# Input projection: one 512-column matmul against the high and low halves of x for the product in bank 3, with the halves added in the gathering

## The chip, the cores and the metric

The kernel runs on one core of a Trainium2 chip. The metric is the device time of one execution in microseconds (us); lower is better. The kernel before takes 1921.91 us (median of three runs, 1921.67 to 1923.59).

## The reference

Two layers are computed for 512 positions of width 2048: a pooling mixer and a multi-head latent attention. The change lies in the first matrix product of the mixer:

```python
def pool_mixer_layer(x, norm_g, w_in, w_group, scale, w_out):
    h = rmsnorm(x, norm_g)
    proj = h @ w_in                      # 512 x 2048 times 2048 x 8192
    u, gate = proj[..., :W_A], proj[..., W_A:]
    ...                                  # causal mean pooling of u in four groups
    y = jnp.einsum('bsgc,gcd->bsgd', pooled, w_group).reshape(B, S, W_A) * scale
    y = y * jax.nn.silu(gate)
    return x + y @ w_out
```

All of it is float32. The kernel keeps that precision with two rounded halves of every operand, high and low, and three products: high weights by high x, high weights by low x, low weights by high x.

## The kernel before, in words

**The input projection** works on *pairs* of output tiles (two times 128 output columns, all 512 positions). It treats a pair and the two halves of the positions (H = 256) as a two-by-two block product and needs seven products instead of eight, of combined weights and combined x (a Strassen-Winograd scheme). Thirty pairs are done this way; two more were done plainly, in the stretch ahead, while the combined x were made.

- `w_combos(pair, q)` loads raw weights, combines them on VectorE (DVE, line 308) and GpSimd (POOL, lines 310 and 311), casts the seven high parts on ScalarE (ACT, line 314: `hi`) and subtracts for the low parts on DVE (line 315: `lo`). `hi` and `lo` have two buffers each, so the cast for one group of weights waits until TensorE (PE) has finished the group two before it. A pair has four such groups, q = 0 to 3; each serves two values of j.
- `seven(ks, w, j)` issues for each of the seven products three matmuls of 256 columns: lines 333 (high weights, high x), 335 (high weights, low x) and 337 (low weights, high x). The table `SEVEN` says which weight, which x, which PSUM bank and which half of that bank. Banks 0, 1 and 2 hold two products each, one in either half. Bank 3 holds one, in half 0, the fourth of the seven; its half 1 stays idle. `ps7` holds two sets of four banks, used by turns.
- `gather(ks, pair)` adds the seven sums: an ACT copy of bank 2's half 0 (line 343), then four DVE additions (lines 344 to 347); line 346 reads bank 3. Pairs are then stored to DRAM, or pooled first (`pool_tile`).

**Behind the last pair** comes the next stage: for each group, products of the pooled tiles (`at`, cast on ACT and subtracted on DVE, line 149) with the group weights (`whi` and `wlo`, lines 126 and 127), matmul lines 144 to 146, 24 of them for each of eight outputs `o`. Each load of weights serves 12 matmuls. DVE also scales the gate tiles read back from DRAM there (line 454). I call the start of the first of these matmuls, right behind the last pair, the *handover*.

**The order** on each engine is set by a scheduler that runs a model of the timeline while the program is built; it places each instruction where its model finds it ready. Engines then work strictly in that order. The code of all stages is scheduled together, so the end of one stage and the start of the next interleave.

Of the kernel before, what the change touches and what calls it, by code (L numbers as in the profile page):

```python
# [11 lines left out]
ALU = mybir.AluOpType  # L12
AX = mybir.AxisListType

P = 128
# [32 lines left out]
def trunk_kernel(  # L48
# [17 lines left out]
    V, A, G, T = nc.vector, nc.scalar, nc.gpsimd, nc.tensor  # L66
# [12 lines left out]
    def at(dt=F32R, shape=(P, S)):  # L79
        return apool.tile(list(shape), dt, tag="a", name="at")  # L80

    def bt(shape=(P, S), dt=F32R):
        return bpool.tile(list(shape), dt, tag="b", name="bt")
# [19 lines left out]
    def dram():  # L103
        return dpool.tile([P, S], F32, tag="scr", name="scr", bufs=64)
# [46 lines left out]
    def gsplit(src, gcol, hi, lo):  # L151
        g = cs[:, gcol:gcol + 1]
        A.activation(hi, src, AF.Copy, scale=g)
        V.scalar_tensor_tensor(lo, src, g, f(hi), ALU.mult, ALU.subtract)
# [73 lines left out]
    H = 256  # L228
    NJ = KD // 2
# [5 lines left out]
    def pool_tile(src, neg, w):  # L235

        up = tt_(PAD + S)
        G.memset(up[:, 0:PAD], 0.0)
        if len(src.shape) == 3:
            dst, r = (a.rearrange("p (h t) -> p h t", h=2) for a in (up[:, PAD:], ra[0]))  # L240
        else:
            dst, r = up[:, PAD:], ra[0]
        V.scalar_tensor_tensor(dst, src, -1.0 if neg else 1.0, r, ALU.mult, ALU.mult)
        prev, off = up, PAD
        m = 1
        while m < w:
            ext = w - 2 * m
            nw = S + ext
            nx = tt_(PAD + S)
            V.tensor_tensor(nx[:, 0:nw], prev[:, off - ext:off + S],  # L250
                            prev[:, off - ext - m:off + S - m], ALU.add)
            prev, off = nx, ext
            m *= 2
        s = prev

        V.scalar_tensor_tensor(s[:, 0:w - 1], s[:, 0:w - 1], float(w), cs[:, C_RCNT:C_RCNT + w - 1],
                               ALU.mult, ALU.mult)
        pl = tt_()
        V.scalar_tensor_tensor(pl, s[:, 0:S], 1.0 / w, up[:, PAD:], ALU.mult, ALU.subtract)
        return pl  # L260

    with ExitStack() as c1:
# [3 lines left out]

        ps7 = [c1.enter_context(tc.tile_pool(name=f"ps7{i}", bufs=1, space=bass.MemoryType.PSUM, **tile_))
               for i in range(2)]
        xh, xl = [None] * NJ, [None] * NJ

        def x_load(j):

# [4 lines left out]
        def x_parts(j, c, hp):  # L277

            nc.sync.dma_start(c[:, 0:2, :], xT[2 * j + 1].rearrange("p (h t) -> p h t", h=2))
            hl = xcp[j].tile([P, 2, 7, H], F32R, tag="xc", name="xc")  # L280
            h, lo = hl[:, 0], hl[:, 1]
            xh[j], xl[j] = h, lo
            h12 = hp.tile([P, H], F32R, tag="h12", name="h12", bufs=NJ)
            l12 = hp.tile([P, H], F32R, tag="l12", name="l12", bufs=NJ)
            gsplit(c[:, 2, :], C_GA + 2 * j, h[:, 2, :], lo[:, 2, :])
            gsplit(c[:, 7, :], C_GA + 2 * j, h12, l12)
            gsplit(c[:, 0:2, :], C_GA + 2 * j + 1, h[:, 0:2, :], lo[:, 0:2, :])
            return h12, l12
# [31 lines left out]
        def banks(n):  # L320
            return [ps7[n % 2].tile([P, 2, H], F32, tag=f"k{i}", name=f"k{i}") for i in range(4)]
# [5 lines left out]
        def seven(ks, w, j):  # L327
            hi, lo = w
            for wi, xi, b, h in SEVEN:
                dst = ks[b][:, h, :]  # L330
                first, last = j == 0 and h == 0, j == NJ - 1

                T.matmul(dst, hi[:, j % 2, wi, :], xh[j][:, xi, :], start=first, stop=False,  # L333
                         skip_group_check=True)
                T.matmul(dst, hi[:, j % 2, wi, :], xl[j][:, xi, :], start=False, stop=False,  # L335
                         skip_group_check=True)
                T.matmul(dst, lo[:, j % 2, wi, :], xh[j][:, xi, :], start=False, stop=last,  # L337
                         skip_group_check=True)

        def gather(ks, pair):  # L340

            e = epool.tile([P, 7, H], F32, tag="e", name="e")
            A.copy(e[:, 6, :], ks[2][:, 0, :])
            V.tensor_tensor(e[:, 0:2, :], e[:, 6:7, :].broadcast_to([P, 2, H]), ks[0], ALU.add)
            V.tensor_tensor(e[:, 2, :], e[:, 1, :], ks[2][:, 1, :], ALU.add)
            V.tensor_tensor(e[:, 3:6:2, :], e[:, 1:3, :], ks[3][:, 0:1, :].broadcast_to([P, 2, H]), ALU.add)
            V.tensor_tensor(e[:, 4:7:2, :], e[:, 2:4, :], ks[1], ALU.add)
            for i, v in enumerate((e[:, 0:7:6, :], e[:, 4:6, :])):
                o = 2 * pair + i
                raws[o] = dram()  # L350
                if i:
                    neg.add(o)
                if o < 8:
                    nc.sync.dma_start(raws[o], pool_tile(v, i == 1, WINS[0]))
                else:
                    nc.sync.dma_start(raws[o].rearrange("p (h t) -> p h t", h=2), v)
# [3 lines left out]
        with ExitStack() as c2:  # L360
            hp = c2.enter_context(tc.tile_pool(name="hp", bufs=2, **tile_))
            for j in range(NJ):
                c4 = ExitStack()
                if j == 0:
                    c4.enter_context(tc.high_priority())
                c = x_load(j)
                raw = hp.tile([P, 4, 2, P], F32, tag="hraw", name="hraw")
                hi = w7.tile([P, 4, 2, P], F32R, tag="hi", name="hi")
                lo = w7.tile([P, 4, 2, P], F32R, tag="lo", name="lo")
                parts = None  # L370
                for m in (0, 2):
                    for o in (m, m + 1):
                        nc.sync.dma_start(raw[:, o, :, :], awin[32 + o][:, 2 * j * P:2 * (j + 1) * P].rearrange(
                            "p (k n) -> p k n", k=2))
                    parts = parts or x_parts(j, c, hp)
                    split(raw[:, m:m + 2], hi[:, m:m + 2], lo[:, m:m + 2])
                h12, l12 = parts
                c4.close()
                x_sums(j, c)
                a, b = xh[j], xl[j]  # L380
                for o in range(4):
                    for dst, k, h, l in ((accs[o][:, 0, :], 0, a[:, 2, :], b[:, 2, :]),
                                         (accs[o][:, 1, :], 0, h12, l12),
                                         (accs[o], 1, a[:, 0:2, :], b[:, 0:2, :])):
                        first = j == 0 and h is not h12 and k == 0
                        T.matmul(dst, hi[:, o, k, :], h, start=first, stop=False, skip_group_check=True)
                        T.matmul(dst, hi[:, o, k, :], l, start=False, stop=False, skip_group_check=True)
                        T.matmul(dst, lo[:, o, k, :], h, start=False, stop=j == NJ - 1 and k == 1,
                                 skip_group_check=True)
        epool = c1.enter_context(tc.tile_pool(name="epool", bufs=2, **tile_))  # L390
        tp[0] = c1.enter_context(tc.tile_pool(name="tpool1", bufs=6, **tile_))
        for o in range(0, 4, 2):
            e = epool.tile([P, 7, H], F32, tag="e", name="e")
# [18 lines left out]
        for n, pair in enumerate((*range(18, 32), *range(16))):  # L412
            ks = banks(n)
            for q in range(NJ // 2):
                w = w_combos(pair, q)
                seven(ks, w, 2 * q)
                seven(ks, w, 2 * q + 1)
            if 0 < n < 9:
                squares(2 * n - 2)
            if n == 9:  # L420
                V.tensor_tensor(sq[0], sq[0], sq[1], ALU.add)
                p = ps7[0].tile([P, 2, H], F32, tag="k3", name="k3").rearrange("p h t -> p (h t)")
                ra[0] = norm_r(sq[0], D, p)
            gather(ks, pair)
# [41 lines left out]
    for g in range(NG):  # L466
# [11 lines left out]
        for o in range(KD):  # L478
            first = len(wloads)
# [15 lines left out]
    for k in range(KD):  # L495
        hi, lo = at(), at()
        gsplit(xr[k], C_GKV + k, hi, lo)
        xkv.append((hi, lo))
        hi, lo = bt(), bt()
# [45 lines left out]
    for k0 in range(0, KD, 4):  # L545
# [7 lines left out]
        for j in range(4):  # L553
            k = k0 + j
            xh, xl = xkv[k]
# [497 lines left out]
    for m in range(len(seq) + 2):  # L1053
        now = seq[m] if m < len(seq) else None
        if now:
            hg, h, i = now
# [26 lines left out]
    for ins in block[begin:]:  # L1083
        e = ins.engine
# [77 lines left out]
```

## Time and profile before

| | before |
|---|---|
| median of three runs | 1921.91 us |
| the profiled execution, its own time | 1925.17 us |
| its span | 1923.4 us |
| granted TensorE clock | 1.00 |
| first matmul of the thirty pairs | 53.8 us |
| first matmul of the next stage | 662.01 us |
| VectorE busy over the span | 66% |
| ScalarE busy over the span | 42% |
| matmuls of lines 333, 335, 337 | 1680 each |

Times of rows count from the span's start. A row of the timeline gives start, duration (both us), engine, line, operation, the tiles written and read, and in brackets how long the engine sat idle before it and what ended that. The span leaves out 1.8 us of the profiled execution's own time.

### The profile page before, as it was taken

How to read it: one execution, taken by the hardware profiler on the slowest of the kernel's cores; microseconds unless marked ns; L12 is line 12 of the kernel's file. 1: busy time of each engine (PE TensorE's matmuls, PEld its weight loads, DVE VectorE, ACT ScalarE, POOL GpSimd, SP SyncE). 2: the span in 40 equal slices, each digit the busy share in tenths (PEclk: the TensorE clock that was granted, in tenths of full speed). 3: DMA queues.
4: the chain of work that ended last, by engine and by line, in shares of the span. 5: the costliest groups of instructions: out<-in, count | busy, mean ns of one | idle time of the engine just before them, and what ended most of it. 6: DMA issues, size and time to landing. Idle time of an engine off the chain costs nothing.

```text
span 1923.4 us, 30647 instructions
## 1 busy us (share of the span) xinstructions
PE 1905.5 (99%) x11324; PEld 1701.2 (88%) x11324; DVE 1277.0 (66%) x2252; ACT 816.1 (42%) x1525; POOL 280.6 (15%) x436
## 2 busy tenths in 40 slices
PE   8999999999999999999999999999999999999999
PEld 7999999999999988888888888888888888988887
DVE  8677785797666777486595566564335988887332
ACT  8443433333333433233333354233235787785221
POOL 0433333343222100000000000000001232320000
PEclk9999999999999999999999999999999999999999
DMA  6454444344444446344344344234343222234632
GB/s 191 154 165 155 153 130 134 121 130 136 147 146 135 159 154 213 116 126 146 112 132 137 105 148 137 89 93 126 118 124 95 82 92 71 81 123 147 202 117 88
DMA packets 177079, 251.27 MB, mean 131 GB/s; under 512 B 15776, under 2 KB 96800, under 8 KB 176928
## 3 DMA queue, kind: packets, MB, share of 16 engines
q1 hardware_dynamic: 176640, 249.10, 41.2%
q8 instruction: 89, 1.46, 0.3%
q14 instruction: 62, 0.51, 0.1%
q10 hardware_dynamic: 288, 0.20, 0.0%
HBM read 216.21 MB, written 33.03 MB: 130 GB/s over the span
## 4 chain that ended last, share of the span: by engine, by line
PE 89%; DVE 4%; DMA 3%; ACT 1%; issue 1%; SPq 0%; POOL 0%; DVEq 0%; ACTq 0%; POOLq 0%
PE mm L144 15%; PE mm L146 15%; PE mm L145 15%; PE k L337 10%; PE k L335 10%; PE k L333 10%; PE sc L789 2%; PE mm L641 1%; PE mm L642 1%; PE mm L643 1%; PE mm L664 1%; PE mm L666 1%; PE mm L665 1%; PE tr L817 1%; PE tr L755 1%
## 5 line engine op out<-in xcount | busy, mean ns | idle before, releaser
L126 ACT CAST whi<-raw 128x512 fp32r<-128x512 f32 (+2 forms) x424 | 255.7, 606 | 514.3 <-PE mm L145 428.8
L333 PE MATMUL k<-xc,hi 128*128 128x256 f32 x1680 | 460.1, 283 | 0.0
L335 PE MATMUL k<-xc,hi 128*128 128x256 f32 x1680 | 460.0, 283 | 0.0
L127 DVE TENSOR_TENSOR wlo<-raw,whi 128x512 fp32r<-128x512 f32 (+2 forms) x424 | 283.3, 669 | 239.5 <-ACT whi L126 236.5
L337 PE MATMUL k<-xc,lo 128*128 128x256 f32 x1680 | 417.8, 283 | 1.6 <-DVE lo L315 1.6
L146 PE MATMUL mm<-bt,wlo 128*128 128x512 f32 x944 | 368.1, 390 | 1.1 <-DVE wlo L127 1.1
L144 PE MATMUL mm<-bt,whi 128*128 128x512 f32 x944 | 367.7, 390 | 0.0
L145 PE MATMUL mm<-bt,whi 128*128 128x512 f32 x944 | 367.2, 389 | 0.0
L314 ACT CAST hi<-raw 128x1792 fp32r<-128x1792 f32 x120 | 202.8, 1690 | 365.0 <-PE k L337 252.8
L315 DVE TENSOR_TENSOR lo<-raw,hi 128x1792 fp32r<-128x1792 f32 x120 | 249.0, 2075 | 158.7 <-ACT hi L314 158.6
L333 PEld LDWEIGHTS k<-xc,hi 128*128 128x128 f32 x1680 | 322.5, 192 | 0.2 <-ACT hi L314 0.2
L335 PEld LDWEIGHTS k<-xc,hi 128*128 128x128 f32 x1680 | 322.5, 192 | 0.0
L337 PEld LDWEIGHTS k<-xc,lo 128*128 128x128 f32 x1680 | 296.8, 192 | 2.7 <-DVE lo L315 2.2
L146 PEld LDWEIGHTS mm<-bt,wlo 128*128 128x128 f32 x944 | 177.2, 188 | 38.8 <-DVE wlo L127 1.5
L144 PEld LDWEIGHTS mm<-bt,whi 128*128 128x128 f32 x944 | 177.3, 188 | 37.1 <-issue 0.2
L145 PEld LDWEIGHTS mm<-bt,whi 128*128 128x128 f32 x944 | 177.3, 188 | 36.3
L145 PE MATMUL mm<-at,whi 128*128 128x512 f32 x432 | 169.0, 391 | 0.6 <-DVE at L149 0.6
L146 PE MATMUL mm<-at,wlo 128*128 128x512 f32 x432 | 168.5, 390 | 0.5 <-DVE wlo L127 0.5
L144 PE MATMUL mm<-at,whi 128*128 128x512 f32 x432 | 168.9, 391 | 0.0
L310 POOL TENSOR_TENSOR raw<-raw 128x256 f32<-128x256 f32 x120 | 98.5, 821 | 436.9 <-DVE raw L308 414.1
L311 POOL TENSOR_TENSOR raw<-raw 128x256 f32<-128x256 f32 x120 | 102.7, 856 | 9.2
L145 PEld LDWEIGHTS mm<-at,whi 128*128 128x128 f32 x432 | 81.1, 188 | 18.6 <-DVE at L149 2.1
(1133 smaller groups left out, 2535.6 us busy)
## 6 DMA issues: line engine op xcount, KB each, us to landing
raw<-awin SPq DMA_DIRECT2D x240, 256.0 KB, 3.3
raw<-awo SPq DMA_DIRECT2D x128, 256.0 KB, 2.8
raw<-bwin SPq DMA_DIRECT2D x80, 256.0 KB, 2.8
raw<-awg SPq DMA_DIRECT2D x64, 256.0 KB, 2.8
scr<-e SPq DMA_DIRECT2D x56, 256.0 KB, 2.7
raw<-bwo SPq DMA_DIRECT2D x56, 256.0 KB, 2.8
raw<-wkvb SPq DMA_DIRECT2D x32, 256.0 KB, 3.0
raw<-wqb SPq DMA_DIRECT2D x32, 192.0 KB, 2.4
```

The costliest lines, as they stand in the source:

```text
L126: A.copy(hi[:, :n], raw[:, :n])
L127: V.tensor_tensor(lo[:, :n], raw[:, :n], f(hi[:, :n]), ALU.subtract)
L144: T.matmul(dst, wh, xh, start=first, stop=False)
L145: T.matmul(dst, wh, xl, start=False, stop=False)
L146: T.matmul(dst, wl, xh, start=False, stop=last)
L310: G.tensor_tensor(c[:, :, 6, :], c[:, :, 4, :], c[:, :, 2, :], ALU.add)
L311: G.tensor_tensor(c[:, :, 7, :], c[:, :, 6, :], c[:, :, 3, :], ALU.add)
L314: A.copy(hi, c[:, :, 1:8, :])
L315: V.tensor_tensor(lo, c[:, :, 1:8, :], f(hi), ALU.subtract)
L333: T.matmul(dst, hi[:, j % 2, wi, :], xh[j][:, xi, :], start=first, stop=False, skip_group_check=True)
L335: T.matmul(dst, hi[:, j % 2, wi, :], xl[j][:, xi, :], start=False, stop=False, skip_group_check=True)
L337: T.matmul(dst, lo[:, j % 2, wi, :], xh[j][:, xi, :], start=False, stop=last, skip_group_check=True)
```

## The change

For bank 3, high weights now meet high and low x in one matmul of 512 columns: the high part fills half 0 of the bank, the low part the half that was idle. The moving operand is `xhl[j][:, :, xi, :]`, two runs of 256 columns from the high and the low half of the x tile, which lie 7 x 256 elements apart. The third matmul (low weights) still adds to half 0. `gather` copies bank 3's half 1 to SBUF on ACT (new line 348), adds half 0 to it on DVE (new line 351), and the addition that read bank 3 (now line 352) reads that sum from SBUF.

```diff
-        xh, xl = [None] * NJ, [None] * NJ
+        xh, xl, xhl = [None] * NJ, [None] * NJ, [None] * NJ
...
-            xh[j], xl[j] = h, lo
+            xh[j], xl[j], xhl[j] = h, lo, hl
...
-                T.matmul(dst, hi[:, j % 2, wi, :], xh[j][:, xi, :], start=first, stop=False,
-                         skip_group_check=True)
-                T.matmul(dst, hi[:, j % 2, wi, :], xl[j][:, xi, :], start=False, stop=False,
-                         skip_group_check=True)
+                if b == 3:
+                    T.matmul(ks[3], hi[:, j % 2, wi, :], xhl[j][:, :, xi, :], start=first, stop=False,
+                             skip_group_check=True)
+                else:
+                    T.matmul(dst, hi[:, j % 2, wi, :], xh[j][:, xi, :], start=first, stop=False,
+                             skip_group_check=True)
+                    T.matmul(dst, hi[:, j % 2, wi, :], xl[j][:, xi, :], start=False, stop=False,
+                             skip_group_check=True)
...
             A.copy(e[:, 6, :], ks[2][:, 0, :])
+            A.copy(e[:, 4, :], ks[3][:, 1, :])
             V.tensor_tensor(e[:, 0:2, :], e[:, 6:7, :].broadcast_to([P, 2, H]), ks[0], ALU.add)
             V.tensor_tensor(e[:, 2, :], e[:, 1, :], ks[2][:, 1, :], ALU.add)
-            V.tensor_tensor(e[:, 3:6:2, :], e[:, 1:3, :], ks[3][:, 0:1, :].broadcast_to([P, 2, H]), ALU.add)
+            V.tensor_tensor(e[:, 4, :], e[:, 4, :], ks[3][:, 0, :], ALU.add)
+            V.tensor_tensor(e[:, 3:6:2, :], e[:, 1:3, :], e[:, 4:5, :].broadcast_to([P, 2, H]), ALU.add)
```

The line numbers move with it: 333, 335 and 337 become 337, 339 and 341, the merged matmul is line 334, the additions 344 to 347 become 349, 350, 352 and 353, the copy of line 343 becomes 347, and all later lines move by six.

Three places show what the scheduler made of it. On TensorE, inside the first group of weights of the first pair (`k_665` to `k_668` are banks 0 to 3), the order was

```order
L333 MATMUL k_667<-xc,hi 128x256
L335 MATMUL k_667<-xc,hi 128x256
L333 MATMUL k_668<-xc,hi 128x256
L335 MATMUL k_668<-xc,hi 128x256
L337 MATMUL k_665<-xc,lo 128x256
L337 MATMUL k_666<-xc,lo 128x256
L337 MATMUL k_667<-xc,lo 128x256
L337 MATMUL k_668<-xc,lo 128x256
```

and is now

```order
L337 MATMUL k_667<-xc,hi 128x256
L339 MATMUL k_667<-xc,hi 128x256
L334 MATMUL k_668<-xc,hi 128x512
L341 MATMUL k_665<-xc,lo 128x256
L341 MATMUL k_666<-xc,lo 128x256
L341 MATMUL k_667<-xc,lo 128x256
L341 MATMUL k_668<-xc,lo 128x256
```

Two matmuls became one, 240 times in all (30 pairs, 8 values of j); the rest of TensorE's order around them stays.

On ScalarE, from the last pair's last two casts to the next stage's first weights (`k_7233` was bank 2 of the last pair; now `k_7060` is its bank 3 and `k_7059` its bank 2), the order was

```order
L314 CAST hi<-raw 128x1792 x2
L149 CAST at<-tt__7487 128x512
L149 CAST at<-tt__7493 128x512
L149 CAST at<-tt__7499 128x512
L149 CAST at<-tt__7505 128x512
L126 CAST whi<-raw 128x512 x3
L343 COPY e<-k_7233 128x256
L149 CAST at<-tt__7511 128x512
L149 CAST at<-tt__7517 128x512
L149 CAST at<-tt__7523 128x512
```

and is now

```order
L314 CAST hi<-raw 128x1792 x2
L149 CAST at<-tt__7307 128x512
L149 CAST at<-tt__7313 128x512
L348 COPY e<-k_7060 128x256
L149 CAST at<-tt__7319 128x512
L149 CAST at<-tt__7325 128x512
L347 COPY e<-k_7059 128x256
L126 CAST whi<-raw 128x512 x3
L149 CAST at<-tt__7331 128x512
L149 CAST at<-tt__7337 128x512
L149 CAST at<-tt__7343 128x512
L149 CAST at<-tt__7349 128x512
```

Both copies of the last gathering, which wait for TensorE's last pair, now stand ahead of the casts of the next stage's first three weight tiles; before, the one copy stood behind them. At the end of every other pair the new copy stands just ahead of a line 314 cast and the old one just behind it.

On VectorE at the same place (`tt__7355` and `tt__7401` are gate tiles being scaled), the order was

```order
L149 TENSOR_TENSOR at<-tt__7505,at 128x512
L127 TENSOR_TENSOR wlo<-raw,whi 128x512 x3
L344 TENSOR_TENSOR e<-e,k_7231 128x512
L454 SCALAR_TENSOR_TENSOR tt__7535<-tt__7535,r 128x512
L149 TENSOR_TENSOR at<-tt__7511,at 128x512
L454 SCALAR_TENSOR_TENSOR tt__7581<-tt__7581,r 128x512
L149 TENSOR_TENSOR at<-tt__7517,at 128x512
```

and is now

```order
L351 TENSOR_TENSOR e<-e,k_7060 128x256
L149 TENSOR_TENSOR at<-tt__7319,at 128x512
L149 TENSOR_TENSOR at<-tt__7325,at 128x512
L349 TENSOR_TENSOR e<-e,k_7057 128x512
L127 TENSOR_TENSOR wlo<-raw,whi 128x512 x2
L350 TENSOR_TENSOR e<-e,k_7059 128x256
L127 TENSOR_TENSOR wlo<-raw,whi 128x512
L460 SCALAR_TENSOR_TENSOR tt__7355<-tt__7355,r 128x512
L149 TENSOR_TENSOR at<-tt__7331,at 128x512
L460 SCALAR_TENSOR_TENSOR tt__7401<-tt__7401,r 128x512
L352 TENSOR_TENSOR e<-e 128x2x256
L149 TENSOR_TENSOR at<-tt__7337,at 128x512
```

The first weight subtractions now stand behind two additions of the last gathering, the `at` subtraction of the fifth pooled tile (`tt__7331`) behind three, and that of the sixth (`tt__7337`) behind all but the last of the five.

## The prediction

> **What bounds the kernel now.** I read the page first: its span, the busy line, the chain and the costliest groups.
>
> ```profile
> span 1923.4 us, 30647 instructions
> PE 1905.5 (99%) x11324; PEld 1701.2 (88%) x11324; DVE 1277.0 (66%) x2252; ACT 816.1 (42%) x1525; POOL 280.6 (15%) x436
> ...
> PE 89%; DVE 4%; DMA 3%; ACT 1%; issue 1%; SPq 0%; POOL 0%; DVEq 0%; ACTq 0%; POOLq 0%
> ...
> L333 PE MATMUL k<-xc,hi 128*128 128x256 f32 x1680 | 460.1, 283 | 0.0
> ```
>
> TensorE is busy 99% of the span and the chain that ended last is its own work. So a matmul saved counts in full, and a microsecond in which TensorE is made to wait counts in full too, wherever it falls. The second view is the busy time by windows, for the pace of 256 columns (first row, inside the thirty pairs) and of 512 (second row, the next stage).
>
> ```profile
> 400.00:500.00 100.00, 100.00 (x835) 100.00 (x834) 79.25 (x79) 35.19 (x25) 38.94 (x44) 1.00 0.44 138
> 900.00:1000.00 100.00, 100.00 (x443) 82.84 (x442) 67.53 (x109) 31.09 (x52) 0.67 (x6) 1.00 0.38 117
> ```
>
> 835 matmuls of 256 columns in 100 us are 119.8 ns each; 443 of 512 columns are 225.7 ns each. The clock is 1.00 in both. Twice 119.8 less 225.7 is 13.9 ns: a part that each matmul costs whatever its width. Third, the waits of TensorE between 50 and 700 us:
>
> ```profile
> PE k L337 <- DVE lo L315: 1.6, 3, 1.1
> ```
>
> In the thirty pairs it waits three times, 1.6 us in all. Weights arrive in time there, so DVE and ACT have room.
>
> **The matmuls removed.** 30 pairs times 8 values of j: 240 times two matmuls of 256 columns become one of 512. The windows give 13.9 ns each. A nearer row is the stretch ahead of the pairs, where both widths alternate on the same x tiles: its period is six matmuls of 256 columns and three of 512. These are the starts of the first 512 of one period and of the one six periods on.
>
> ```profile
> 44.65 0.40 PE L386 MATMUL k<-xc,hi 128*128 128x512 f32 x1
> ...
> 53.09 0.40 PE L386 MATMUL k<-xc,hi 128*128 128x512 f32 x1
> ```
>
> 8.44 us by six is 1.407 us; twelve matmuls of 256 columns would take 12 x 119.8 = 1.438. Three merges save 0.031 us, 10.3 ns each. I take 11.5 ns, nearer the mixed row: 240 x 11.5 = **2.8 us saved**, 2.5 to 3.3 by the two rows. No row shows a moving operand in two runs. At worst the second run pays the fixed part again and the merge saves nothing; that is the low end, 0.
>
> [...]
>
> **The gathering at the end of a pair.** What it gains is an ACT copy (line 348) and a DVE addition (351). First ACT, then DVE, around the pair that ends at 460.4:
>
> ```profile
> 460.61 1.69 ACT L314 CAST hi<-raw 128x1792 fp32r<-128x1792 f32 x1 [3.34 <-PE k L337]
> 462.20 0.36 ACT L343 COPY e<-k 128x256 f32<-128x256 f32 x1
> ```
>
> ```profile
> 462.34 2.02 DVE L315 TENSOR_TENSOR lo<-raw,hi 128x1792 fp32r<-128x1792 f32 x1 [1.90 <-ACT hi L314]
> 464.28 0.69 DVE L308 TENSOR_TENSOR raw<-raw 128x512 f32<-128x512 f32 x1
> 464.88 0.68 DVE L344 TENSOR_TENSOR e<-e,k 128x512 f32<-128x512 f32 x1
> 465.60 0.42 DVE L345 TENSOR_TENSOR e<-e,k 128x256 f32<-128x256 f32 x1
> ```
>
> The new copy stands ahead of the cast at 460.61. It waits for bank 3's last product, and bank 3 is the fourth product of seven, so nine matmuls (9 x 0.12 = 1.08 us) ahead of the pair's end. The cast waits for the pair's end anyway, with 3.34 us of idle time ahead of it. The copy, 0.36 us like line 343, starts 1.08 us earlier than the cast and is done before it: no cost. The addition, 0.42 us like line 345, falls into the 1.90 us in which DVE waits for that cast: no cost. Line 352 reads SBUF alone; the nearest row is line 308, as wide and in SBUF alone, 0.69 us, what line 346 takes. Without this cover each pair would pay 0.4 us, 12 us in all.
>
> The cover is thin where DVE also pools: the subtraction at 439.04 ends at 441.05, and TensorE uses it at 441.20.
>
> ```profile
> 439.04 2.01 DVE L315 TENSOR_TENSOR lo<-raw,hi 128x1792 fp32r<-128x1792 f32 x1
> ...
> 441.20 0.65 PE L337 MATMUL k<-xc,lo 128*128 128x256 f32 x4
> ```
>
> An addition of 0.42 us ahead of it, not all absorbed, could cost 0.2 us. Near 269 us, where the norm is computed among the subtractions, one of the three waits stands; the new order puts that subtraction ahead of part of the gathering, which may win about as much back. I cost both at **nothing**, give or take 0.4.
>
> **The handover.** Here both copies moved ahead of casts that TensorE needs at once. The last product of the last pair, the next stage's first matmul, and its 25th:
>
> ```profile
> 661.89 0.28 PE L337 MATMUL k<-xc,lo 128*128 128x256 f32 x1
> 662.01 0.40 PE L144 MATMUL mm<-at,whi 128*128 128x512 f32 x1
> ...
> 668.47 0.40 PE L144 MATMUL mm<-at,whi 128*128 128x512 f32 x1
> ```
>
> Call 662.01 T. Before, TensorE runs on without a gap, and 24 matmuls take 6.46 us. ACT before:
>
> ```profile
> 657.65 1.23 ACT L126 CAST whi<-raw 128x512 fp32r<-128x512 f32 x2 [1.75 <-DMA raw<-awg]
> 659.27 0.62 ACT L126 CAST whi<-raw 128x512 fp32r<-128x512 f32 x1 [0.40 <-DMA raw<-awg]
> 662.21 0.37 ACT L343 COPY e<-k 128x256 f32<-128x256 f32 x1 [2.31 <-DMA tt__7581<-scr]
> 662.48 0.62 ACT L149 CAST at<-tt__7511 128x512 fp32r<-128x512 f32 x1
> 663.00 0.62 ACT L149 CAST at<-tt__7517 128x512 fp32r<-128x512 f32 x1
> ```
>
> The weights are cast by 659.9. The copy waits for the pair's end: it starts 0.32 us behind the last matmul's start. The next instruction follows a copy after 0.27 us and a cast after 0.52. With these steps in the new order: copy 348 at T - 0.12 - 1.08 + 0.32 = T - 0.88; two `at` casts at T - 0.61 and T - 0.09; copy 347 at T + 0.43; the first weight cast at T + 0.70, done at T + 1.32. TensorE **stands still from T to about T + 1.4**.
>
> DVE is worse. Its rows before, with steps of 0.60 us between two such instructions:
>
> ```profile
> 662.61 0.69 DVE L344 TENSOR_TENSOR e<-e,k 128x512 f32<-128x512 f32 x1 [2.00 <-DMA raw<-awg]
> 663.22 0.69 DVE L454 SCALAR_TENSOR_TENSOR tt__7535<-tt__7535,r 128x512 f32<-128x512 f32 x1
> 663.82 0.69 DVE L149 TENSOR_TENSOR at<-tt__7511,at 128x512 fp32r<-128x512 f32 x1
> ...
> 665.03 0.68 DVE L149 TENSOR_TENSOR at<-tt__7517,at 128x512 fp32r<-128x512 f32 x1
> ```
>
> Now: `at` subtractions at T + 0.04 and 0.64, addition 349 at 1.24, first `wlo` at 1.84, done at 2.53; TensorE's third matmul waits for it to T + 2.6. Then `wlo` 2.44, addition 350 at 3.04, `wlo` 3.37, scaling 3.97, the fifth tile's subtraction 4.57, scaling 5.17, addition 352 at 5.77, the sixth tile's subtraction at 6.37, done at T + 7.05; before, this one stood at 665.03 = T + 3.02. The sixth tile's second matmul (the 17th) waits for it, to T + 7.1. Eight more steps of 0.228 bring the 25th matmul to T + 8.9, against T + 6.46: **2.5 us lost**, by DVE's chain. Behind it, all that follows is as late as TensorE, so nothing is regained; the end moves by the same.
>
> One transfer could add to this. The first gate tile is read when the third tile's subtraction is done, now at T + 0.73, before 4 us ahead of T. Medians from issue to landing, of that tile and of the one with the least:
>
> ```profile
> tt__7535<-scr SPq DMA_DIRECT2D x1, 256.0 KB, 4.5
> ...
> tt__7627<-scr SPq DMA_DIRECT2D x1, 256.0 KB, 2.6
> ```
>
> Issued at T + 0.8 it lands between T + 3.4 and T + 5.3; DVE reaches the scaling at T + 3.97. At 4.5 us the handover costs 3.8 us rather than 2.5. Few other transfers are under way then, so I take the short one. The low end is 0, if more is hidden than I see.
>
> **The sum** is -2.8 + 2.5 = -0.3 us. The profiled execution's own 1925.17 (span 1923.4 and 1.8 around it) would become 1924.9. It lies 3.3 us above the median of the runs, 1921.91; the same step from the median gives **1921.6 us**.
>
> **The rivals.**
> - *The handover is nearly free.* For it: TensorE waited little there before. Against: the order shows the copies ahead of the casts, and the copies cannot start before the last pair's products. The merges alone: 1921.91 - 2.8 = 1919.1, 1918.6 at best.
> - *The merged matmul saves nothing*, because its operand's second run pays the fixed part again. For it: no row shows two runs. Against: the head's 512 columns do save, from the same tiles in one run. The handover is left: 1921.91 + 2.5 = 1924.4. [...]
> - *Slower: the gate tile is late.* It decides from a landing behind T + 3.97, 3.2 us after its issue; each us behind that is a us lost, because the fifth, sixth, seventh and eighth tile's subtractions queue behind the scaling. At 4.5 us: -2.8 + 3.8, so 1922.9. For a loss of over 0.2% it would have to land over 7 us after issue, more than any row here shows.
> - *That no merge happens* is excluded by the order: 240 matmuls of 512 columns stand there.
>
> **How the numbers follow.** The forecast gets 0.55, the free handover 0.17, the merge that saves nothing 0.14, the late tile 0.14. 0.2%, about what a measurement of this kernel can tell from no change, is 3.8 us: below 1918.1 or above 1925.7. Even the merges alone, at 3.3 us, don't reach the first, so 0.05 for faster; a useless merge with a late tile (+3.8) just reaches the second, so 0.07 for slower; 0.88 for no change. The range runs from the free handover to the useless merge: 1918.9 to 1924.8.
>
> **What would show it.** Right: about 225 to 230 ns from each merged matmul to the next, the last pair's end some 2.8 us earlier (near 659.2), then a wait of TensorE for the first `whi` of about 1.4 us, waits for a `wlo` and for the sixth `at`, and the 25th matmul of the next stage 8.9 us behind the last pair's end. Wrong: new waits of line 341 for line 315 at every pair's end, a merged matmul near 240 ns, or a handover without waits.

## The result, and the profile after

The changed kernel takes 1926.79 us (median of 22 executions, 1924.18 to 1929.49), the kernel before 1923.79 us beside it (22 executions, 1921.67 to 1928.78): a ratio of **1.0015, 95% interval 1.0009 to 1.0021**, so 1.7 to 4.0 us slower. The forecast was 1921.6 us within 1918.9 to 1924.8. Measured by differences, -0.3 us was forecast and +3.0 came. The profiled execution took 1926.28 us, 1.11 more than the profiled one of before (1925.17).

The page of the kernel after: its span, the busy line, the chain by engines, and one group of the new matmuls' neighbours.

```profile
span 1924.4 us, 30226 instructions
PE 1906.0 (99%) x11084; PEld 1688.9 (88%) x11084; DVE 1302.1 (68%) x2282; ACT 827.8 (43%) x1555; POOL 288.1 (15%) x436
...
PE 90%; DVE 4%; DMA 3%; ACT 2%; issue 1%; SPq 0%; POOL 0%; DVEq 0%; ACTq 0%; POOLq 0%
...
L337 PE MATMUL k<-xc,hi 128*128 128x256 f32 x1440 | 396.8, 282 | 0.0
```

240 matmuls fewer (11084 against 11324), and 240 each gone from the two lines of high weights (1440 against 1680). Yet TensorE is busy 0.5 us longer. Its waits between 50 and 700 us (total, times, longest), after:

```profile
PE mm L144 <- ACT whi L126: 1.2, 1, 1.2
PE k L341 <- DVE lo L315: 0.5, 2, 0.3
PE mm L146 <- DVE wlo L127: 0.5, 1, 0.5
```

The first and the third are the handover's; before, TensorE waited there for no `whi`, and for a `wlo` once, 0.53 us at 688.98. TensorE's rows around it, after: the first product of the thirty pairs, the last one, then matmuls of the next stage.

```profile
53.54 0.28 PE L337 MATMUL k<-xc,hi 128*128 128x256 f32 x1
...
659.14 0.28 PE L341 MATMUL k<-xc,lo 128*128 128x256 f32 x1
660.63 0.50 PE L144 MATMUL mm<-at,whi 128*128 128x512 f32 x1 [1.21 <-ACT whi L126]
...
661.84 0.50 PE L146 MATMUL mm<-at,wlo 128*128 128x512 f32 x1 [0.48 <-DVE wlo L127]
...
662.88 0.63 PE L144 MATMUL mm<-at,whi 128*128 128x512 f32 x1
663.31 0.63 PE L145 MATMUL mm<-at,whi 128*128 128x512 f32 x1
...
666.29 0.39 PE L146 MATMUL mm<-at,wlo 128*128 128x512 f32 x1
...
668.60 0.39 PE L144 MATMUL mm<-at,whi 128*128 128x512 f32 x1
```

The last pair ends at T = 659.14 + 0.12 = 659.26; before it was 662.01. The first matmul behind it starts at T + 1.37 and the third at T + 2.58 (computed: 1.4 and 2.6). The 25th, the last row, starts at T + 9.34 instead of T + 6.46. So 2.75 us were won up to T and 2.88 lost right behind it. From the 25th matmul to the end the execution took 0.9 us longer than before, 1255.85 against 1254.91, in stages whose code the edit does not touch. Between 662.88 and 666.29 the matmuls stand 0.43 us apart instead of 0.23, which the prediction did not have. The prediction had read the first 24 of before as running without a gap. They held three short stops: their 6.46 us are 1.0 more than 24 x 0.228. The longest, at the 23rd, before:

```profile
667.90 0.50 PE L145 MATMUL mm<-at,whi 128*128 128x512 f32 x1 [0.24 <-DVE at L149]
```

ACT after, then DVE after:

```profile
658.37 0.37 ACT L348 COPY e<-k 128x256 f32<-128x256 f32 x1 [6.24 <-PE k L341]
...
659.68 0.37 ACT L347 COPY e<-k 128x256 f32<-128x256 f32 x1
659.95 1.67 ACT L126 CAST whi<-raw 128x512 fp32r<-128x512 f32 x3
```

```profile
660.51 0.68 DVE L349 TENSOR_TENSOR e<-e,k 128x512 f32<-128x512 f32 x1
661.11 1.28 DVE L127 TENSOR_TENSOR wlo<-raw,whi 128x512 fp32r<-128x512 f32 x2
...
663.24 0.68 DVE L460 SCALAR_TENSOR_TENSOR tt__7355<-tt__7355,r 128x512 f32<-128x512 f32 x1
...
665.65 0.68 DVE L149 TENSOR_TENSOR at<-tt__7337,at 128x512 fp32r<-128x512 f32 x1
```

Copy 348 stands at T - 0.89 (computed T - 0.88), the weight casts at T + 0.69 (0.70), the first `wlo` at T + 1.85 (1.84), the sixth tile's subtraction at T + 6.39 (6.37). The gate tile's scaling (line 460) did not wait.

### The profile page after: what moved, and what is told of

It reads as the page before. It is cut to its first block, busy times and chain, and to the rows that moved or that the text cites. A ratio compares the mean times of both kernels' runs of the same rounds, so it can differ in the third digit from the quotient of the medians.

```text
span 1924.4 us, 30226 instructions
## 1 busy us (share of the span) xinstructions
PE 1906.0 (99%) x11084; PEld 1688.9 (88%) x11084; DVE 1302.1 (68%) x2282; ACT 827.8 (43%) x1555; POOL 288.1 (15%) x436
## 4 chain that ended last, share of the span: by engine, by line
PE 90%; DVE 4%; DMA 3%; ACT 2%; issue 1%; SPq 0%; POOL 0%; DVEq 0%; ACTq 0%; POOLq 0%
PE mm L146 15%; PE mm L144 15%; PE mm L145 15%; PE k L341 10%; PE k L339 9%; PE k L337 9%; PE k L334 3%; PE sc L795 2%; PE mm L647 1%; PE mm L670 1%; PE mm L649 1%; PE mm L648 1%; PE mm L672 1%; PE mm L671 1%; PE tr L823 1%
## 5 line engine op out<-in xcount | busy, mean ns | idle before, releaser
L339 PE MATMUL k<-xc,hi 128*128 128x256 f32 x1440 | 397.5, 283 | 0.0
L337 PE MATMUL k<-xc,hi 128*128 128x256 f32 x1440 | 396.8, 282 | 0.0
L341 PEld LDWEIGHTS k<-xc,lo 128*128 128x128 f32 x1680 | 302.7, 190 | 8.3 <-DVE lo L315 2.0
L337 PEld LDWEIGHTS k<-xc,hi 128*128 128x128 f32 x1440 | 273.3, 190 | 5.0
L339 PEld LDWEIGHTS k<-xc,hi 128*128 128x128 f32 x1440 | 273.7, 190 | 0.0
L310 POOL TENSOR_TENSOR raw<-raw 128x256 f32<-128x256 f32 x120 | 97.6, 813 | 426.9 <-DVE raw L308 411.7
L311 POOL TENSOR_TENSOR raw<-raw 128x256 f32<-128x256 f32 x120 | 110.9, 924 | 9.2
L146 PEld LDWEIGHTS mm<-at,wlo 128*128 128x128 f32 x432 | 81.5, 189 | 18.6 <-DVE wlo L127 1.3
```

Of the source, the lines that this page charges most:

```text
L146: T.matmul(dst, wl, xh, start=False, stop=last)
L310: G.tensor_tensor(c[:, :, 6, :], c[:, :, 4, :], c[:, :, 2, :], ALU.add)
L311: G.tensor_tensor(c[:, :, 7, :], c[:, :, 6, :], c[:, :, 3, :], ALU.add)
```

## The experiments

**Theory A**: the loss sits in the handover; the merges gain, though less than forecast. **Theory B**: the loss sits in the thirty pairs, in the merged matmuls or the longer gathering. Two numbers are read from each trace. The first is the time of a *quarter* of a pair: the matmuls of one group of weights, two values of j, 42 before and 40 after. Quarters are counted from 0 through the thirty pairs; from 80 to 110, where nothing waits, all thirty agree within 0.003 us. Before, the first row of quarter 80 and of quarter 110:

```profile
460.41 0.28 PE L333 MATMUL k<-xc,hi 128*128 128x256 f32 x1
...
611.61 0.28 PE L333 MATMUL k<-xc,hi 128*128 128x256 f32 x1
```

151.20 / 30 = 5.040 us. After, a merged matmul of quarter 80, the four low products behind it, and the merged matmul at the same place of quarter 110:

```profile
458.91 0.40 PE L334 MATMUL k<-xc,hi 128*128 128x512 f32 x1
459.15 0.64 PE L341 MATMUL k<-xc,lo 128*128 128x256 f32 x4
459.62 0.28 PE L337 MATMUL k<-xc,hi 128*128 128x256 f32 x1
...
609.71 0.40 PE L334 MATMUL k<-xc,hi 128*128 128x512 f32 x1
```

150.80 / 30 = 5.027 us. Two merges save 13.3 ns, so **6.6 ns each** where 11.5 were counted, 120 quarters 1.6 us. The second number is the start of the 25th matmul of the next stage behind the last pair's end (6.46 before, 9.34 after).

| kernel | ratio to before, 95% interval | quarter, us | 25th behind T, us |
|---|---|---|---|
| before | 1 | 5.040 | 6.46 |
| the change | 1.0015 (1.0009 to 1.0021) | 5.027 | 9.34 |
| the change again | 1.0018 (1.0008 to 1.0027) | 5.027 | 9.30 |
| last pair as before | 0.9999 (0.9990 to 1.0008) | 5.027 | 6.46 |
| the same again | 0.9998 (0.9989 to 1.0006) | 5.027 | 6.47 |
| last pair alone changed | 1.0012 (1.0003 to 1.0021) | 5.040 | 9.08 |
| x halves adjacent | 1.0021 (1.0012 to 1.0030) | 5.027 | 9.30 |
| products apart, new gathering | 1.0026 (1.0014 to 1.0037) | 5.040 | 9.07 |
| banks 3 and 2 first | 1.0010 (1.0001 to 1.0019) | 5.027 | 8.60 |
| side by side, last as before | 0.9988 (0.9979 to 0.9997) | 5.007 | 6.47 |
| side by side, all thirty | 1.0003 (0.9994 to 1.0012) | 5.007 | 9.28 |
| order alone | one run, 1926.47 us | 5.040 | 6.47 |
| low product between | one run, 1920.63 us | 5.007 | 6.48 |
| bank 3 first, last as before | 0.9988 (0.9979 to 0.9997) | 5.020 | 6.47 |
| bank 3 last | one run, 1931.13 us | 5.027 | 9.27 |

**The last pair as before**, and the same again beside the change:

```diff
-                if b == 3:
+                if b == 3 and merge:
...
-            gather(ks, pair)
+            gather(ks, pair, n < 29)
```

(`merge` is n < 29 in `seven` too, and in `gather` it chooses between the old and the new additions.)

> 29 pairs merged and gathered as in the change, the last pair (n = 29) as before. The copies of the last pair then stand behind the weight casts again. Theory A (the loss sits in the handover, the merges save 6.5 to 11.5 ns each): 232 merges save 1.5 to 2.7 us, the handover costs nothing, so 1.5 to 2.7 us less than before (ratio 0.9986 to 0.9992); first matmul of the next stage within 0.2 us of the last pair's end, no 427 ns spacing there. Theory B (the loss sits in the thirty pairs: the merged matmuls or the longer gathering): still 2 to 3 us more than before (1.0010 to 1.0015).

> 29 pairs merged, the last as before, again, beside the change itself. Theory A: 2.5 to 3.7 us less than the change, 0 to 1.5 us less than before. Theory B: as the change.

> The change itself again, on the same chip and in the same rounds as the next two. Theory A: 1.7 to 4 us more than before, the 25th matmul 9.2 to 9.5 us behind the last pair's end, as in its first trace, and again matmuls 427 ns apart in the next stage. If the slow matmuls were a chance event of one execution, they are absent here.

The last pair's one copy stands behind the weight casts again. Its rows at the handover:

```profile
659.30 0.28 PE L341 MATMUL k<-xc,lo 128*128 128x256 f32 x1
659.42 0.40 PE L144 MATMUL mm<-at,whi 128*128 128x512 f32 x1
...
665.88 0.39 PE L144 MATMUL mm<-at,whi 128*128 128x512 f32 x1
```

No wait, and the 25th at 6.46 us behind the first. Measured side by side, the change takes 1926.11 us and this kernel 1923.38, 2.7 less, so theory B falls. Against before, though, only 0.2 and 0.4 us are gained, with some 1.7 us either way, where 1.5 at least was expected: the interval just reaches that, no more.

**The last pair alone**, 29 pairs as before (`n == 29` in place of `n < 29`):

> Only the last pair merged and gathered as in the change, the other 29 as before. Theory A: the handover alone, 2.9 us by the trace of the change, 3.6 with the wait that came 90 us later: 2.5 to 3.7 us more than before (1.0013 to 1.0019). Theory B: within 0.5 us of before.

```profile
660.65 0.28 PE L341 MATMUL k<-xc,lo 128*128 128x256 f32 x1
662.14 0.50 PE L144 MATMUL mm<-at,whi 128*128 128x512 f32 x1 [1.21 <-ACT whi L126]
...
663.36 0.50 PE L146 MATMUL mm<-at,wlo 128*128 128x512 f32 x1 [0.49 <-DVE wlo L127]
...
667.90 0.50 PE L145 MATMUL mm<-at,whi 128*128 128x512 f32 x1 [0.84 <-DVE at L149]
...
669.85 0.39 PE L144 MATMUL mm<-at,whi 128*128 128x512 f32 x1
```

Here stand all three waits that the prediction computed, the third (the 17th matmul, for the sixth tile's `at`) at T + 7.13 against 7.1, and the 25th at T + 9.08 against 8.9. 1.0012 is 2.3 us (0.6 to 4.0), for a change in one pair of thirty; at least 2.5 was expected. Theory A holds. The extra 0.7 us that was put into the upper end of the expectation, for a wait 90 us later, did not show: the matmuls from the 25th to the last took 1248.07 us here and 1250.32 before, in one profile each.

**The products apart, the gathering new**: two matmuls of 256 columns into the two halves of bank 3.

```diff
-                    T.matmul(ks[3], hi[:, j % 2, wi, :], xhl[j][:, :, xi, :], start=first, stop=False,
+                    T.matmul(ks[3][:, 0, :], hi[:, j % 2, wi, :], xh[j][:, xi, :], start=first, stop=False,
...
+                    T.matmul(ks[3][:, 1, :], hi[:, j % 2, wi, :], xl[j][:, xi, :], start=False, stop=False,
```

> The change's gathering in all thirty pairs, but the two products of bank 3 as two matmuls of 256 columns into its two halves. Takes the merge alone away. By the spacings in the trace of the change (6.5 ns a merge): 1.6 us more than the change, 4.6 more than before (1.0024). By 11.5 ns: 2.8 more than the change, 5.8 more than before (1.0030). If the merges save nothing: as the change (1.0015). The stage of the thirty pairs then shows what the gathering alone costs: against before, 608.2 us less the 0.8 us of waits that fell, if it is hidden.

1.0026 is 5.0 us, near the 4.6 that 6.6 ns a merge give, and the quarter is back at 5.040. The agreement of the time is in part luck, for the merge is not all that went. The gathering is not hidden in the middle of the pairs: quarters 37 to 76 take 3.3 us more here than 40 times 5.040. Before it was 1.3 more, so in this kernel the gathering costs 2.0 us; after it was 1.9 more than 40 times 5.027. The quarter, not the time, shows the 6.6 ns. The waits for `lo` between 200 and 450 us, in this kernel, then after, then before:

```profile
PE k L343 <- DVE lo L315: 1.3, 3, 0.6
```

```profile
PE k L341 <- DVE lo L315: 0.3, 1, 0.3
```

```profile
PE k L337 <- DVE lo L315: 0.2, 1, 0.2
```

**The two runs of the operand.** The x tile is laid out as `[P, 7, 2, H]`, so that the merged operand is one run of 512 columns; the 512-column operands ahead of the pairs become two runs.

```diff
-            hl = xcp[j].tile([P, 2, 7, H], F32R, tag="xc", name="xc")
-            h, lo = hl[:, 0], hl[:, 1]
+            hl = xcp[j].tile([P, 7, 2, H], F32R, tag="xc", name="xc")
+            h, lo = hl[:, :, 0], hl[:, :, 1]
```

> The change, with the high and the low half of each combination of x next to each other, so that the merged operand is one run of 512 columns; the 512-column operands of the stretch ahead of the pairs become two runs instead. Theory A1 (the second run of the operand costs the 5 ns by which a merged matmul saves less than in the one-run stretch): from a merged matmul to the next 228 ns instead of 233 to 241, the pairs 1.2 us shorter; ahead of the pairs 96 operands pay 5 ns, 0.5 us; in all 0.7 us less than the change, 2.3 more than before (1.0012). Theory A2 (the spacing does not depend on the runs but on what follows the merged matmul): spacing stays at 233 to 241, the time that of the change (1.0015).

The quarter stays at 5.027: the second run costs nothing, and A1 falls. The time, 1.0021, can't be told from the change's. The stretch ahead of the pairs, 47.38 us, lies among the others' 46.3 to 47.8.

**Side by side.** In 29 pairs the merged matmuls of two neighbouring j follow each other; the last pair is as before.

```diff
+                if merge and j > j0:
+                    for k in (j0, j):
+                        T.matmul(ks[3], hi[:, k % 2, 3, :], xhl[k][:, :, 4, :], start=k == 0, stop=False,
...
+                    for k in (j0, j):
+                        T.matmul(ks[3][:, 0, :], lo[:, k % 2, 3, :], xh[k][:, 4, :], start=False,
```

> As the run with the last pair as before, but in the other 29 pairs the merged matmuls of two neighbouring j stand side by side (merged, merged, then the two low products), instead of one merged matmul between matmuls of 256 columns each. A quarter of a pair (two j) took 5.040 us before and 5.027 with two merges apart. Theory C (each change of width, 256 to 512 and back, costs some 7 ns, which is why a merge saves 6.6 ns and not 11.5): a quarter takes 5.019 to 5.020, 116 quarters save 0.9 us more than the run with the merges apart. Theory D (a merged matmul itself is 7 ns longer here than in a stage of 512 columns only): 5.027, no further gain. In both the handover is that of before (25th matmul of the next stage 6.5 us behind the last pair's end).

```profile
458.06 0.28 PE L342 MATMUL k<-xc,hi 128*128 128x256 f32 x1
...
458.78 0.63 PE L333 MATMUL k<-xc,hi 128*128 128x512 f32 x2
459.25 0.51 PE L346 MATMUL k<-xc,lo 128*128 128x256 f32 x3
459.59 0.28 PE L342 MATMUL k<-xc,hi 128*128 128x256 f32 x1
...
608.26 0.28 PE L342 MATMUL k<-xc,hi 128*128 128x256 f32 x1
```

150.20 / 30 = 5.007: two merges save 33 ns, more than twice the 13.9 ns that the prediction estimated from its two windows. Neither theory foresaw that. The merged matmuls themselves still take 0.47 / 2 = 0.235 us, so theory C's price for a change of width is not it; the gain comes behind them, where three low products take 0.34 us instead of 0.36. At 0.9988 (0.9979 to 0.9997) this kernel **beats both**, the one before by 2.3 us, with an interval that just excludes none. Two controls, one run each, take the order apart: the same order with the merged matmuls split in two (first), and the low product of the first j between the merged ones again (second).

> The side-by-side order of the run before, with the gathering of the change in 29 pairs, but each merged matmul replaced by two of 256 columns. A quarter of a pair took 5.040 us before, 5.007 with two merged matmuls side by side. If the gain of that run comes from the merged matmuls standing together: 5.040 here. If the order alone gave part of it: 5.020 here.

> As the side-by-side run, but in each quarter the low product of the first j stands between the two merged matmuls again, and the scheduler moves the first one further ahead. Theory C' (what pays is that two merged matmuls follow each other directly): 5.027 us a quarter, as with the merges apart in the change. Theory G (what pays is where in the quarter they stand): 5.007.

5.040 and 5.007: the order alone gains nothing in the quarter, and the two need not be neighbours. C' falls, G stands.

**Side by side in all thirty pairs**, the last among them:

> The merged matmuls side by side in all thirty pairs, the last among them, so that the copies stand ahead of the weight casts at the handover again, while the last pair's bank 3 is finished 18 matmuls ahead of its end. Theory A: the handover costs again, 25th matmul 8.5 to 9.2 us behind the last pair's end, 2 to 2.7 us more than the run that keeps the last pair as before (ratio to before 0.9998 to 1.0003); a quarter 5.007 us. Theory B: as that run (0.9988).

The handover is back (25th at 9.28), and with it 1924.09 us against the 1921.05 of the kernel that differs in the last pair alone: 3.0 us.

**Banks 3 and 2 first** in the last j of the last pair, all thirty merged:

```diff
+                seven(ks, w, 2 * q + 1, SEVEN if n < 29 or q < 3 else [SEVEN[i] for i in (3, 0, 6, 1, 4, 2, 5)])
```

> The change with all thirty pairs merged; only in the last j of the last pair the products of banks 3 and 2 come first, those of banks 0 and 1 last, so that the two copies are not held up to the pair's end. Computed as in the prediction: copy 348 at T - 2.0, copy 347 at T - 0.65, first weight cast done at T + 0.8, first low weights at T + 2.0, the sixth tile's subtraction done at T + 5.9, 25th matmul at T + 7.8 instead of the change's T + 9.3: 1.5 us less than the change. If the handover's loss did not hang on those copies, the 25th matmul would stay at T + 9 and the time at the change's.

The 25th comes at T + 8.60, 0.7 us earlier than in the change, not 1.5, and 0.2 to 0.3 of that is the slow stretch of the change, which did not come here (last section). The time is 0.6 less (1925.55 against 1926.11), too little to tell from none. Two things were missed. The scheduler interleaved the products again, so that bank 2 was finished 0.36 us ahead of the pair's end and copy 347 stood at T - 0.16 instead of T - 0.65, as ACT's row shows (the pair ends at 659.26):

```profile
659.10 0.37 ACT L347 COPY e<-k 128x256 f32<-128x256 f32 x1 [0.39 <-PE k L341]
```

And with the sixth tile earlier, the seventh was late as well: TensorE waited 0.24 us for each. In the trace the direction holds, by 0.5 us against the 9.07 and 9.08 of the two kernels without the slow stretch; nothing but the order of the last products was changed.

**Where bank 3 stands in the list.** First in `SEVEN`, and last, both with the last pair as before:

```diff
-        SEVEN = ((2, 0, 0, 0), (0, 6, 1, 0), (1, 2, 2, 0), (3, 4, 3, 0),
+        SEVEN = ((3, 4, 3, 0), (2, 0, 0, 0), (0, 6, 1, 0), (1, 2, 2, 0),
```

> 29 pairs merged, the last as before; the list of the seven products begins with bank 3, all else as in the run with the last pair as before. In the first j of a quarter the merged matmul then stands ahead of the six other high products (not between them and four low ones), in the second ahead of its own low product. Theory P (only the merged matmul that four low products follow gains nothing, each other gains 13 to 20 ns): a quarter takes 5.007 to 5.014 us instead of 5.027, 1.5 to 2.3 us less over 116 quarters; ratio to before 0.9985 to 0.9992 with the handover of before. Theory Q (the first merged matmul of a quarter gains nothing wherever it stands unless a second one or three low products follow): 5.027, ratio 0.9995 to 1.0000.

> As the run before, but with bank 3 last in the list of seven. The scheduler again puts the first merged matmul of a quarter behind six high products, but only three low ones follow, the fourth (bank 3's own) comes later. Theory P: 5.007 us a quarter. Theory Q': the place in the list does not matter, 5.027.

First, in two rows 30 quarters apart:

```profile
458.53 0.40 PE L334 MATMUL k<-xc,hi 128*128 128x512 f32 x1
...
609.13 0.40 PE L334 MATMUL k<-xc,hi 128*128 128x512 f32 x1
```

150.60 / 30 = 5.020, between P and Q. Last: 5.027, so the three low products of P are not the reason. The cause of the place's effect stays open. The run with bank 3 last has a second lesson, for its last pair is neither merged nor gathered in the new way, and still its handover cost 2.8 us (25th at 9.27): the one old copy moved ahead of the weight casts.

```profile
663.57 0.37 ACT L347 COPY e<-k 128x256 f32<-128x256 f32 x1 [6.47 <-PE k L341]
663.84 0.62 ACT L149 CAST at<-tt__7331 128x512 fp32r<-128x512 f32 x1
664.36 1.66 ACT L126 CAST whi<-raw 128x512 fp32r<-128x512 f32 x3
```

So the order alone makes this loss, without the added work. The rest of that run's 1931.13 us lies in part in the pairs, in waits for `lo` (3.3 us against 1.6 before) and a slow stretch behind one of them (last section). Bank 3 first differs from the run "last pair as before" by one line, and takes 1921.50 us, 0.9988 (0.9979 to 0.9997) of before.

## Why the prediction was wrong

The mechanism of the loss was forecast with its parts; the sum failed on sizes. Of the 3.3 us between the forecast difference of -0.3 and the measured +3.0, the merges account for 1.2, the handover for 0.4, the gathering for some 0.3, and 1.4 stay open.

- **The merges: the step that failed.** 240 x 11.5 ns = 2.8 us were counted, 240 x 6.6 = 1.6 came. Both rows behind the 11.5 compare stretches with several wide matmuls in succession; a lone wide one among narrow ones is a case that neither showed, so the value belonged further down in its own bounds of 0 to 3.3 us. The rival "a merged matmul near 240 ns" was half right: from the trace's starts, one of the two in a quarter takes 241 ns to the next and gains nothing, the other 233. The reason given for it, the operand's second run, is refuted: the quarter is 5.027 us with two runs and with one.
- **The sign that deceived.** The last pair was to end near 659.2, and did, at 659.26. But of those 2.75 us the merges gave 1.6; 0.25 is the earlier start of the pairs (53.79 to 53.54), and the remaining 0.9 is less waiting for `lo`, with the refilling behind each wait (1.6 us of waiting in the row of before, 0.5 in that of after; the four low products behind the longest wait, at 61.28 us of before, take 0.58 us to the next start, those at 642.81, without a wait, 0.48). The profiled execution of before had waited 1.4 us of that in the first quarters, where one changed kernel waited 0.2 and the same kernel in another execution 0.9.
- **The gathering**: costed at 0, give or take 0.4. The waits for `lo` and their refilling in quarters 37 to 76 add 1.3 us to the quarters before and 1.3 to 1.9 in six traces with the change's merges and gathering. So 0 to 0.6 us by these waits, at the edge of what was allowed, and 0.8 to 2.2 in the kernels with another order of the products or with the products apart. The cover was thin where the prediction said, and thinner than it costed.
- **The handover**: 2.5 us forecast, 2.62 with the clock at 1.00 (last pair alone: 9.08 - 6.46) and 2.88 in the change. The cause is shown: taken away in the last pair alone it goes, put there alone it comes. ACT's and DVE's steps came within 0.03 us of the sum. What was missed is the clock, below.
- **The late gate tile** did not happen, the **free handover** neither.
- **The base**: the three runs shown had a median of 1921.91, the 22 runs 1923.79. The 1921.6 carries that difference of 1.9 us besides its own error.

The measured terms are -1.6, +0.3 (the middle of 0 to 0.6) and +2.9, in all +1.6 us. The runs say +3.0, within 1.7 to 4.0, so 1.4 us are not settled. Summed in the same way, nine of ten measurements of kernels with the new gathering in 29 or 30 pairs lie 0.4 to 2.7 us above the terms of their own traces, and the kernel with the last pair alone 0.2 below. So the gathering may cost about 1 us more than its waits in the traces show; that is not shown, for each measurement has some 1.7 us either way. The executions differ by as much in places that no edit touches: the matmuls from the 25th on took 1248.07 to 1253.37 us in one profile each, without any relation to the order at the handover.

## What to carry to other kernels

An edit inside a loop of thirty also edits the last turn, and there the work that it adds has no cover: a scheduler placed two short copies ahead of the next stage's first casts, and one turn lost more (2.9 us) than all the turns had won (1.6). With the last turn left as it was the loss went, unless another order of the products moved a copy ahead of the casts again: look at the engines' order at the boundary after every edit. A saving per instruction is read from a stretch with the same neighbours, not from a stretch of the same width; where the trace has none, the place in the order is worth trying, for it moved the gain of two merges from 13 to 33 ns.

## What the runs showed of the hardware

**The clock after short waits.** Two neighbouring windows of 3.41 us at the handover in the change (the third number from the right is the granted clock), then in the kernel with the last pair alone changed:

```profile
659.44:662.85 3.41, 1.74 (x6) 1.16 (x7) 3.41 (x7) 3.41 (x8) 0.00 (x0) 1.00 0.52 155
662.85:666.26 3.41, 3.41 (x9) 2.64 (x8) 3.41 (x7) 2.09 (x4) 0.00 (x0) 0.50 0.81 241
```

```profile
658.94:662.35 3.41, 2.20 (x17) 1.95 (x16) 1.96 (x4) 2.46 (x6) 0.00 (x0) 1.00 0.02 7
662.35:665.77 3.42, 2.93 (x13) 2.07 (x12) 3.42 (x7) 2.85 (x6) 0.00 (x0) 1.00 0.85 252
```

Eight matmuls from 662.88 to 666.29 stood 0.427 us apart, 3.41 us in all, at a granted clock of 0.50; behind them, at 1.00, they stand 0.23 apart. It happened in both executions of the change, with x halves adjacent, with side by side in all thirty and with bank 3 last: the mean clock from 660 to 670 us was 0.83 in each. With the last pair alone, with the products apart and with banks 3 and 2 first, after waits of the same kind, it did not: 1.00 there. In the run with bank 3 last, whose clock over the whole span was 0.998 against 0.999 in the other four executions, another such stretch stood behind a wait of 1.80 us for `lo` at 61.6 us. At the handover it cost 0.2 to 0.3 us (25th at 9.27 to 9.34 against 9.07 and 9.08), because part of the slow stretch would have been a wait anyway (0.84 us, with the last pair alone).

In the 3.41 us ahead of the slow stretch TensorE was busy 1.74 us in the change, behind two waits. With the last pair alone it was busy 2.20 us in the window shown, and the second wait came in the next. But in the change another window, 3.41 us from 1727.81, had it busy 1.84 us, and the one behind it stayed at 1.00. What decides whether the clock falls was not shown.

**The pace of narrow matmuls.** Quarters came at 5.040, 5.027, 5.020 and 5.007 us, the same to 0.003 us thirty times over: 13, 7 and 13 ns apart, by where the wide matmuls stand, and not by their operand's layout (5.027 with one run as with two).
